# Gated linear attention within chunks: 64x64 blocks on row and column tiles, the inner levels collected at half width

## The chip, the cores and the metric

One core of a Trainium2 chip runs the whole layer in one launch. The metric is device time in microseconds (us), the median of several executions. Before the change it is 1183.76 us (three runs, 1183.09 to 1184.44).

## The reference, cut to what matters

The kernel computes one layer: a token mixer (gated linear attention, GLA, beside a short convolution), an output projection, and a convolutional FFN. The change concerns the attention within chunks of the GLA. For a forward and a backward direction the reference has, with `b` the running sum of the log decays of a chunk:

```python
decay = jnp.exp(jnp.where(mask, b[:, :, None] - b[:, None, :], -jnp.inf))
att = jnp.einsum('bihk,bjhk,bijhk->bijh', qc, kc, decay)
o_intra = jnp.einsum('bijh,bjhv->bihv', att, vc)
```

The decay depends on the channel `k`, so `att` is no single matmul of q and k. There are 1024 tokens, 4 heads, 64 key channels and 128 value channels a head. The kernel works in chunks of 128 tokens.

## The kernel before, in words

**Levels.** A pair of tokens (i, j) of one chunk belongs to the level s of `LEVELS` = 64, 32, 16, 8, 4, 2, 1 at which i and j lie in two neighbouring blocks of s tokens; pairs with i = j are an eighth level, 0. At its own level, the decay from j to i is split at the border of the two blocks into a factor for q and one for k. `level_prep` (L859) makes, for one half of the tokens (4 chunks, 512 columns) and one level, the scaled operands `ql` (tile eq) and `kl` (tile ek): four differences on VectorE (DVE, L867, L868, L875, L876), two exponentials on ScalarE (ACT, through the helper `act`, L127), a product of eq with q on DVE (L882), and the product of ek with k in four parts on GpSimd (POOL, L881). The level with s = 1 needs eq alone, level 0 neither. Tiles eq, ek and eb share a tag with four buffers, so that one level's operands can be made while the level before is multiplied.

**Matmuls.** `level_dot` (L885) multiplies a level: for each of two pairs of chunks (`cp_`) eight matmuls (L894), one for each chunk, each half `fb` of the four heads and each head `hh` in it, with 64 channels on the contraction side and a full block of 128x128 tokens as result. Heads with `hh` 0 and 1 lie on partitions 0 to 63 and 64 to 127, and write two PSUM banks. A result of 128x128 contains products that belong to other levels. The first level is copied whole by ACT into the tile att; each later one is laid over it by a masked copy (`copy_predicated`, DVE, L901), in which the mask of the level picks its own pairs. `out` (L922) then multiplies att with v (L927) and the scaled q with the state (L928), squares on ACT, reduces on DVE, and scales.

**Order.** The order on PE (TensorE) is that of the program. Two generators take turns: `gla` (the attention) and `stream` (blocks of 128 columns of the input projection; "S" below, L144 to L146, 128x512 matmuls on weights in a high and a low part). Each `yield` of the one is followed by one step of the other, twelve S matmuls. A level gives two yields, one after each pair of chunks. Weights of the stream are loaded by the queue of SyncE (SP), copied to their high part wh on ACT and to their low part wl on POOL in four pieces (L634), one block ahead. Beside that run on DVE the recurrence of the states (`recur`, L850, updates of the tile su, 64x128 each, four a chunk) and the short convolution (sc, L676 to L687). The order on DVE, ACT and POOL in this stage is made by a scheduler from the program's order and dependencies; once made, each of these engines runs its own queue in order.

**Stages.** The stage treated here has two halves of tokens (`hf`). Each half runs eight levels and then four `out` steps. Ahead of it the decays are summed (with the matrices tri) and the chunk updates made; behind it follow the last S matmuls, the output projection (w_out) and the FFN.

## Time and profile before

| what | us |
|---|---|
| median of three runs | 1183.76 |
| profiled execution | 1187.9 |
| its span, first to last instruction | 1186.1 |
| levels of the first half, window 247.1 to 317.4 | 70.3 |
| outputs of the first half, to 335.9 | 18.5 |
| levels of the second half, to 401.0 | 65.1 |
| outputs of the second half, to 420.0 | 19.0 |
| L894 busy in the first and the second half's levels | 19.99 and 18.45 |
| masked copies L901 busy in the same windows | 19.23 and 18.88 |

The windows were set by hand at the first matmul of the first level and of the first output of each half. A row of the timeline has start, length, engine, line, operation, output and inputs, shape and count; entries of one kind that follow each other are merged, and in square brackets stands how long the engine was idle before, and who released it. A row of instructions by tile or line has the shortest, median and longest duration in ns. Names are those of the program's tiles without buffer numbers. PEld is the loading of weights into TensorE, PE the matmuls.

### The profile page before, as it was taken

How to read it: one execution, taken by the hardware profiler on the slowest of the kernel's cores; microseconds unless marked ns; L12 is line 12 of the kernel's file. 1: busy time of each engine (PE TensorE's matmuls, PEld its weight loads, DVE VectorE, ACT ScalarE, POOL GpSimd, SP SyncE). 2: the span in 40 equal slices, each digit the busy share in tenths (PEclk: the TensorE clock that was granted, in tenths of full speed). 3: DMA queues.
4: the chain of work that ended last, by engine and by line, in shares of the span. 5: the costliest groups of instructions: out<-in, count | busy, mean ns of one | idle time of the engine just before them, and what ended most of it. 6: DMA issues, size and time to landing. Idle time of an engine off the chain costs nothing. (4 is left out here: it accounts for less than half of the span.)

```text
span 1186.1 us, 15908 instructions
## 1 busy us (share of the span) xinstructions
PE 1150.9 (97%) x5770; PEld 946.1 (80%) x5770; DVE 878.3 (74%) x1215; ACT 518.5 (44%) x931; POOL 479.0 (40%) x467
## 2 busy tenths in 40 slices
PE   8899999999999979999999999999999999999997
PEld 6689967877887868888787788888888888888885
DVE  4965547898769445559688987878787887777676
ACT  5745155643234145556343333333434254544453
POOL 3111001334355201114877776877686871000002
PEclk9999999999999989999999999999999999999999
DMA  9884854311102163232233442233223259978672
GB/s 347 269 293 136 266 153 134 121 57 46 54 18 75 60 217 129 107 125 71 76 101 100 134 141 71 90 125 116 85 79 125 95 161 326 361 246 278 215 241 98
DMA packets 80128, 176.19 MB, mean 149 GB/s; under 512 B 9809, under 2 KB 21585, under 8 KB 80050
## 3 DMA queue, kind: packets, MB, share of 16 engines
q1 hardware_dynamic: 80050, 175.19, 44.4%
q8 instruction: 45, 0.74, 0.3%
q14 instruction: 33, 0.27, 0.1%
HBM read 142.38 MB, written 32.78 MB: 148 GB/s over the span
## 5 line engine op out<-in xcount | busy, mean ns | idle before, releaser
L1296 DVE SCALAR_TENSOR_TENSOR y<-u,cols,y 128x945 f32<-128x945 f32 (+2 forms) x176 | 214.8, 1222 | 3.7 <-ACT y L127 1.3
L144 PE MATMUL ps<-mx,p 128*128 128x512 f32 x440 | 173.6, 395 | 2.9 <-ACT p L127 1.7
L145 PE MATMUL ps<-mx,p 128*128 128x512 f32 x440 | 173.0, 393 | 0.0
L146 PE MATMUL ps<-mx,p 128*128 128x512 f32 x440 | 172.7, 392 | 0.0
L134 POOL TENSOR_TENSOR p<-rs,p 128x512 fp32r<-128x512 f32 x88 | 116.3, 1326 | 88.8 <-ACT p L127 85.0
L146 PE MATMUL ps<-p,p 128*128 128x512 f32 x308 | 120.1, 390 | 0.2
L145 PE MATMUL ps<-p,p 128*128 128x512 f32 x308 | 120.0, 389 | 0.0
L144 PE MATMUL ps<-p,p 128*128 128x512 f32 x308 | 119.9, 389 | 0.0
L634 POOL TENSOR_TENSOR wl<-wr,wh 128x256 fp32r<-128x256 f32 x64 | 52.7, 854 | 159.3 <-ACT wh L127 159.2
L144 PE MATMUL ps<-hxh,wh 128*128 128x512 f32 x256 | 107.5, 420 | 0.0
L229 DVE CUSTOM_DVE_ANT_0 ada<-ada,cb 128x1024 f32<-128x1024 f32 x64 | 79.9, 1263 | 34.2 <-DMA ada<-in_ada 34.1
L144 PEld LDWEIGHTS ps<-mx,p 128*128 128x128 f32 x440 | 82.6, 188 | 25.8 <-ACT u L127 5.0
L146 PE MATMUL ps<-hxh,wl 128*128 128x512 f32 x256 | 101.4, 396 | 0.0
L145 PE MATMUL ps<-hxl,wh 128*128 128x512 f32 x256 | 101.0, 394 | 0.0
L146 PEld LDWEIGHTS ps<-mx,p 128*128 128x128 f32 x440 | 82.6, 188 | 18.6
L127 ACT ACTIVATE p<-rs 128x512 fp32r<-128x512 f32 x88 | 54.5, 622 | 98.0 <-POOL rs L1155 98.0
L145 PEld LDWEIGHTS ps<-mx,p 128*128 128x128 f32 x440 | 82.6, 188 | 18.3
L134 POOL TENSOR_TENSOR p<-wr,p 128x512 fp32r<-128x512 f32 x58 | 76.2, 1314 | 13.1 <-ACT p L127 13.1
L127 ACT ACTIVATE y<-u,cols 128x1024 f32<-128x1024 f32 x22 | 26.6, 1210 | 106.1 <-DVE u L1358 106.1
L144 PE MATMUL ps<-b,p 128*128 128x512 f32 x176 | 69.6, 396 | 0.0
L145 PE MATMUL ps<-b,p 128*128 128x512 f32 x176 | 69.4, 395 | 0.0
L146 PE MATMUL ps<-b,p 128*128 128x512 f32 x176 | 69.4, 394 | 0.0
(271 smaller groups left out, 2636.0 us busy)
## 6 DMA issues: line engine op xcount, KB each, us to landing
ada<-in_ada SPq DMA_DIRECT2D x64, 512.0 KB, 4.6
wr<-in_wu SPq DMA_DIRECT2D x48, 512.0 KB, 4.0
h<-hd SPq DMA_DIRECT2D x77, 256.0 KB, 4.3
hd<-h SPq DMA_DIRECT2D x73, 256.0 KB, 2.1
wdr<-in_wd SPq DMA_DIRECT2D x55, 256.0 KB, 4.0
wdr<-in_wd SPq DMA_DIRECT2D x22, 512.0 KB, 6.1
x<-in_x SPq DMA_DIRECT2D x16, 512.0 KB, 5.5
wr<-in_wb SPq DMA_DIRECT2D x16, 512.0 KB, 3.7
```

Source lines behind the costliest of these rows:

```text
L127: return S.activation(o, i, fn, **kw)
L134: (eng or V).tensor_tensor(lo, raw, hi.bitcast(F32), ALU.subtract)
L144: PE.matmul(ps, lh, rh, start=first, stop=False, skip_group_check=more)
L145: PE.matmul(ps, lh, rl, start=False, stop=False, skip_group_check=more)
L146: PE.matmul(ps, ll, rh, start=False, stop=last, skip_group_check=more)
L229: V.tensor_tensor_reduce(raw, raw, cbs[which], 1.0, 0.0, ALU.mult, ALU.add, dst)
L634: eng.tensor_tensor(lo[:, k : k + 2], raw[:, k : k + 2], hi[:, k : k + 2].bitcast(F32), ALU.subtract)
L1296: V.scalar_tensor_tensor(y3[:, ro, co], u3[:, ri, ci], col("wcf", 9 * p + 3 * (dr_ + 1) + dc + 1), y3[:, ro, co], ALU.mult, ALU.add)
```

## The change

The result of a level is no longer made as 128x128 blocks. Each block is cut into four of 64x64, and only those are computed that the level has pairs in: for level 64 the two off the diagonal (tokens j in one half of the chunk, i in the other), for all others the two on it. One matmul has 64 channels, 64 key tokens and 64 query tokens; the channels' partitions select one of two row tiles of the array, the half `b` of the key tokens one of two column tiles and the output partitions 0 to 63 or 64 to 127. All 32 matmuls of a level are one group, followed by two yields, so 24 S matmuls stand between two groups where 12 stood between two half groups.

The two banks of a level are now full with useful blocks of half width. Level 64 is copied by ACT in four copies of 64 partitions to its places in att; level 32 is copied by ACT whole into a new tile own, which holds the diagonal blocks at half width; the six levels below are laid over own by masked copies, two a half and level; after the last level `whole` copies own into the diagonal places of att in four ACT copies. The masks shrink to 6x64 columns. tri moves from the pool pkq to pgt, which is released at the second step of `kx_turn`, before the first load of the output weights.

```diff
-                for cp_ in range(2):
-                    pts = [bank(ps_at if cp_ == 0 else ps_mm) for _ in range(2)]
...
-                                PE.matmul(pts[hh][:, o : o + P], kl[r, fb, cs], ql[r, fb, cs], start=True, stop=True)
...
-                            V.copy_predicated(dst, masks[:, li - 1, :].unsqueeze(1).broadcast_to([P, H, P]), src)
-                    yield
+            def level_dot(li, kl, ql, att, own):
+                pts = [bank((ps_at, ps_mm)[li % 2]) for _ in range(2)]
+                for n in range(8):
+                    c, fb = n // 2, n % 2
+                    for b in range(2):
+                        ks, qs = (slice(c * P + DK * i, c * P + DK * i + DK) for i in (b, b if li else 1 - b))
+                        for hh in range(2):
+                            r = slice(hh * DK, hh * DK + DK)
+                            PE.matmul(pts[hh][b * DK : b * DK + DK, n * DK : n * DK + DK], kl[r, fb, ks], ql[r, fb, qs],
+                                      start=True, stop=True)
+                for hh in range(2):
+                    src = pts[hh].rearrange("p (a n t) -> p a n t", a=2, t=DK)
+                    if li > 1:
+                        m = masks[:, li - 2, :].unsqueeze(1).unsqueeze(1).broadcast_to([P, 2, 4, DK])
+                        V.copy_predicated(own[:, :, hh], m, src)
+                    elif li == 1:
+                        act(own[:, :, hh], src)
+                    else:
+                        for b in range(2):
+                            r = slice(b * DK, b * DK + DK)
+                            act(att[r, :, hh, :, (1 - b) * DK : (2 - b) * DK], src[r])
+
+            def whole(att, own):
+                for b in range(2):
+                    r = slice(b * DK, b * DK + DK)
+                    for a in range(2):
+                        act(att[r, a, :, :, b * DK : b * DK + DK], own[r, a])
...
-                    yield from level_dot(li, *cur, atts)
+                    level_dot(li, *cur, att, own)
+                    yield
...
+                    if li == len(levels) - 1:
+                        whole(att, own)
+                    yield
```

Where this moves instructions: On PE, in the first level of the first half, eight matmuls of the attention (L894) stood together before S went on; the last two and the first three of S (one hh writes the bank ps_2432, the other ps_2433):

```order
L894 MATMUL ps_2432<-eq_2382,ek_2386 128x128
L894 MATMUL ps_2433<-eq_2382,ek_2386 128x128
L144 MATMUL ps_2404<-hxh_516,wh_2264 128x512
L145 MATMUL ps_2404<-hxl_517,wh_2264 128x512
L146 MATMUL ps_2404<-hxh_516,wl_2265 128x512
```

At the same place of PE's order in the changed kernel, where 32 stand together (all lines lie one or two lower in the file):

```order
L896 MATMUL ps_2432<-eq_2382,ek_2386 64x64
L896 MATMUL ps_2433<-eq_2382,ek_2386 64x64
L145 MATMUL ps_2404<-hxh_516,wh_2264 128x512
L146 MATMUL ps_2404<-hxl_517,wh_2264 128x512
L147 MATMUL ps_2404<-hxh_516,wl_2265 128x512
```

The S matmuls of the same bank follow a group four times as long, of blocks a quarter the size; the second group of eight, which stood behind the next twelve S, is gone.

On DVE, in the first half, the place of level 16's operands (third level; eq_2491 before, eq_2505 now) among the updates of the states su and the convolution's sc. Before:

```order
L854 SCALAR_TENSOR_TENSOR su_1933<-su_1933,dec 64x128 x4
L854 SCALAR_TENSOR_TENSOR su_1932<-su_1933,dec,su_1932 64x128 x4
L854 SCALAR_TENSOR_TENSOR su_1932<-su_1932,dec 64x128 x4
L854 SCALAR_TENSOR_TENSOR su_1931<-su_1932,dec,su_1931 64x128
L686 TENSOR_TENSOR sc_2312<-sc_2312,ps_2404 128x512
L854 SCALAR_TENSOR_TENSOR su_1931<-su_1932,dec,su_1931 64x128 x3
L854 SCALAR_TENSOR_TENSOR su_1931<-su_1931,dec 64x128
L867 TENSOR_TENSOR eq_2491<-bc_1712 128x32x16
```

Now, behind the same first row, where eq_2598 is the fourth level's operand:

```order
L868 TENSOR_TENSOR eq_2505<-bc_1712 128x32x16
L869 TENSOR_TENSOR eq_2505<-bc_1713 128x32x16
L876 TENSOR_TENSOR ek_2509<-bc_1712 128x32x16
L877 TENSOR_TENSOR ek_2509<-bc_1713 128x32x16
L855 SCALAR_TENSOR_TENSOR su_1932<-su_1933,dec,su_1932 64x128
L687 TENSOR_TENSOR sc_2312<-sc_2312,ps_2404 128x512
L883 TENSOR_TENSOR eq_2505<-eq_2505,qh_698 128x1024
L855 SCALAR_TENSOR_TENSOR su_1932<-su_1933,dec,su_1932 64x128 x3
L855 SCALAR_TENSOR_TENSOR su_1932<-su_1932,dec 64x128 x4
L855 SCALAR_TENSOR_TENSOR su_1931<-su_1932,dec,su_1931 64x128 x4
L855 SCALAR_TENSOR_TENSOR su_1931<-su_1931,dec 64x128
L868 TENSOR_TENSOR eq_2598<-bc_1712 128x64x8
```

Level 16's differences moved ahead of thirteen su updates, one of which now stands ahead of their product and twelve between the product and the differences of level 8.

On ACT, at the copies of the first two levels of the first half, behind the copies of ps_2432 and ps_2433 into att. Before:

```order
L127 ACTIVATE att_2418<-ps_2458 128x512
L127 ACTIVATE att_2418<-ps_2459 128x512
L127 ACTIVATE eq_2491<-eq_2491 128x1024
L127 ACTIVATE ek_2495<-ek_2495 128x1024
L127 ACTIVATE wh_2544<-wr_2542 128x1024
L127 ACTIVATE eq_2572<-eq_2572 128x1024
L127 ACTIVATE ek_2576<-ek_2576 128x1024
```

Now, where eq_2505 and ek_2509 are the third level's operands and eq_2598 and ek_2602 the fourth's:

```order
L128 ACTIVATE eq_2505<-eq_2505 128x1024
L128 ACTIVATE ek_2509<-ek_2509 128x1024
L128 ACTIVATE own_2418<-ps_2518 128x2x256
L128 ACTIVATE own_2418<-ps_2519 128x2x256
L128 ACTIVATE eq_2598<-eq_2598 128x1024
L128 ACTIVATE wh_2578<-wr_2576 128x1024
L128 ACTIVATE ek_2602<-ek_2602 128x1024
```

The stream's copy wh moved from between the third and the fourth level's exponentials to between the two exponentials of the fourth. On POOL nothing changes place: the four pieces of wl still stand between the ek products of the third level and those of the fourth.

More of the change, by code (lines that the diff above doesn't have):

```diff
@@ L920, in out_prep, with out @@
                 return qx
-            def out(c, qx, atts):
+            def out(c, qx, att):
                 c4 = c % 4
@@ L926, in out @@
                     hs = slice(h * DV, (h + 1) * DV)
[L927 removed]
+                    PE.matmul(po[:, hs], att[:, c4 // 2, h % 2, 2 * (c4 % 2) + h // 2, :], vt[c][:, hs], start=True, stop=False)
                     PE.matmul(po[:, hs], qx[:, h, :], slot(c)[:, hs], start=False, stop=True)
@@ L945, in gla @@
                     wo_raw(5)
-                atts = [pe_.tile([P, 2, 2, 2, P], F32, tag="att", bufs=2, name=nm("att")) for _ in range(2)]
+                att = pe_.tile([P, 2, 2, 4, P], F32, tag="att", bufs=1, name=nm("att"))
+                own = pe_.tile([P, 2, 2, 4, DK], F32, tag="own", bufs=1, name=nm("own"))
                 for li in range(len(levels)):
@@ L964, in gla @@
                         nxt = level_prep(1, levels[0])
-                    out(4 * hf + c4, qx, atts)
+                    out(4 * hf + c4, qx, att)
                     qx = qn
```

25 lines of the change are left out of this document (6 added, 19 removed).

## The prediction

> **What bounds the kernel now.** I began with the page: span, busy times, and the row of granted clock.
>
> ```profile
> span 1186.1 us, 15908 instructions
> PE 1150.9 (97%) x5770; PEld 946.1 (80%) x5770; DVE 878.3 (74%) x1215; ACT 518.5 (44%) x931; POOL 479.0 (40%) x467
> PEclk9999999999999989999999999999999999999999
> ```
>
> PE carries the kernel, and in the slice that starts at 267 us the clock dips. The change touches only the GLA stage, so the next view is the table by stage: the eight levels of the first half of the tokens, its outputs, the eight levels of the second half, its outputs.
>
> ```profile
> 247.10:317.40 70.30, 67.91 (x449) 53.20 (x449) 63.74 (x104) 23.19 (x26) 30.62 (x41) 0.95 0.16 46
> 317.40:335.90 18.50, 18.50 (x115) 16.12 (x115) 10.41 (x18) 6.20 (x9) 8.01 (x13) 1.00 0.09 29
> 335.90:401.00 65.10, 65.10 (x455) 51.06 (x456) 49.50 (x70) 21.30 (x25) 30.11 (x39) 1.00 0.20 58
> 401.00:420.00 19.00, 19.00 (x115) 16.70 (x114) 9.22 (x17) 4.22 (x7) 5.25 (x8) 1.00 0.25 70
> ```
>
> The columns after the length are PE, PEld, DVE, ACT, POOL, then clock, DMA share and GB/s. PE is full in the second half (65.10 of 65.10) and nearly so in the first; DVE is at 63.74 of 70.30 there. So time that PE saves comes off the end, as long as DVE, ACT and POOL deliver the next level's operands in time. The timeline of PE shows how one group of the attention stands in the stream of 128x512 matmuls ("S" from here on).
>
> ```profile
> 343.84 1.16 PE L894 MATMUL ps<-eq,ek 64*128 64x128 f32 x16
> 344.93 0.50 PE L144 MATMUL ps<-hxh,wh 128*128 128x512 f32 x1
> 345.27 0.39 PE L145 MATMUL ps<-hxl,wh 128*128 128x512 f32 x1
> ...
> 347.56 0.39 PE L146 MATMUL ps<-hxh,wl 128*128 128x512 f32 x1
> 347.88 1.16 PE L894 MATMUL ps<-eq,ek 64*128 64x128 f32 x16
> ```
>
> Ten S steps lie between 345.27 and 347.56, 0.229 us each, twelve are 2.75 us. A group recurs every 4.04 us (343.84 to 347.88), so the eight matmuls of L894 cost 1.29 us. The trace has two entries for each of them (x16). One entry lasts 272 ns (row below), so the 16 start within 1.16 - 0.27 = 0.89 us, 0.056 us apiece; the other 0.40 us is the turn from S to the attention's form and back.
>
> ```profile
> L894 PE MATMUL ps<-eq,ek x384: 272/272/579, 247.1 to 381.1; 64*128 64x128 f32 x192
> 317.88 0.39 PE L927 MATMUL ps<-v,att 128*128 128x128 f32 x2
> 318.10 0.39 PE L928 MATMUL ps<-su,qx 128*128 128x128 f32 x2
> ```
>
> L927 and L928 use all 128 rows: one matmul of two entries each 0.22 us (317.88 to 318.10), 0.11 us an entry, twice the 0.056 us of L894. The two 64-row halves therefore already run side by side, and an entry takes as long as 128 columns need.
>
> The first half has one stall, in the timeline of PE, and it is paid twice:
>
> ```profile
> 259.18 1.16 PE L894 MATMUL ps<-eq,ek 64*128 64x128 f32 x16
> ...
> 265.69 2.60 PE L894 MATMUL ps<-eq,ek 64*128 64x128 f32 x16 [2.40 <-DVE att L901]
> ...
> 273.08 1.16 PE L894 MATMUL ps<-eq,ek 64*128 64x128 f32 x16
> ```
>
> From 259.18 to 265.69 is 6.51 us, 2.47 over the 4.04, a wait for masked copies in DVE's full queue that free the PSUM banks. From 265.69 to 273.08 is 7.39, another 3.35 over, since the clock went down behind the gap (next fence). The stall costs **5.8 us**.
>
> ```profile
> 260.00:270.00 10.00, 7.61 (x40) 6.10 (x37) 9.96 (x15) 3.17 (x4) 6.23 (x8) 0.78 0.11 28
> 270.00:280.00 10.00, 10.00 (x61) 7.71 (x60) 9.20 (x14) 4.73 (x5) 3.55 (x6) 0.88 0.18 53
> ```
>
> **The change, part by part.** *Matmuls.* A level becomes one group of 32 matmuls (64 entries) instead of two of 8 (32 entries). The four 64x64 tiles are two row tiles times two column tiles. The trace shows row tiles side by side and no column tiles, so an entry is bounded: 0.014 us if all four run at once and time goes with columns (half of 0.056 for half the columns, half again for the second pair), and 0.056 us if PE can start none faster than the trace ever shows. I take 0.014, because the row pair runs fully side by side and 128-column entries show no fixed cost beyond their columns: two entries of one 128-column matmul take 0.22 us, an S step of four times the columns 0.229. Then the 64 entries take 0.89 us, and with one turn of 0.40 a level costs 1.29 us instead of 2.58: **16 levels x 1.29 = 20.6 us less**. The level's period goes from 8.08 to 24 x 0.229 + 1.29 = 6.79 us.
>
> Against this stands a rule of the Trainium skill, "TensorE: Matmul & The Clock Gate", section "Back-to-back issue gap": matmuls of 1 to 64 columns follow one another no closer than about 25 ns. By it 64 entries would take 1.6 us, an estimate from that page, and a level 2.0 instead of 1.29; the time is given with the second rival below.
>
> *Evictions.* By level and half four copies become two:
>
> ```profile
> L901 DVE COPY_PREDICATED att<-masks,ps x56: 716/730/747, 264.8 to 398.2; 128x512 f32<-128x512 uint8 x56
> L127 ACT ACTIVATE att<-ps x8: 577/590/598, 248.3 to 343.2; 128x512 f32<-128x512 f32 x8
> L127 ACT ACTIVATE su<-ps x14: 573/592/597, 217.0 to 246.3; 64x512 f32<-64x512 f32 x14
> ```
>
> The 56 masked copies become 24 of the same 512 elements, so DVE loses 32 x 0.73 = 23.4 us. ACT gets 8 copies of 64x512 for level 0 (as many as before; 0.59 by the su row), 4 of 0.59 for level 1 and 8 of about 0.59 that put the diagonal blocks into att: 12 x 0.59 = 7 us on an engine that is busy 23.19 of 70.30. I cost these at nothing. The last four stand between the last level and the first output matmul: two masked copies and four ACT copies are 1.46 + 2.36 = 3.8 us, beneath 24 S steps (5.5 us). If DVE came over 1.7 us late to them, PE would wait for the rest.
>
> *The old stall* goes: level 1's copies are ACT's now, so level 2's successors no longer wait for DVE's queue. **5.8 us less.**
>
> *What is late next.* Level 3's ek. In DVE's queue level 2's four differences and product now come right behind the su update that ended at 254.95, and twelve su updates stand between them and level 3's. Durations:
>
> ```profile
> 253.77 1.18 DVE L854 SCALAR_TENSOR_TENSOR su<-su,dec 64x128 f32<-64x128 f32 x4
> ...
> 257.40 0.69 DVE L686 TENSOR_TENSOR sc<-sc,ps 128x512 f32<-128x512 f32 x1
> ...
> 259.30 0.69 DVE L867 TENSOR_TENSOR eq<-bc 128x512 f32<-128x512 f32 x1
> ...
> 261.72 1.23 DVE L882 TENSOR_TENSOR eq<-eq,qh 128x1024 f32<-128x1024 f32 x1
> ```
>
> ```profile
> L854 DVE SCALAR_TENSOR_TENSOR su<-su,dec 64x128 f32<-64x128 f32 x20 | 8.7, 506 | 0.1
> L854 DVE SCALAR_TENSOR_TENSOR su<-su,dec,su 64x128 f32<-64x128 f32 x16 | 5.3, 393 | 0.0
> ```
>
> An su update is (8.7 + 5.3) / 36 = 0.39 us, four differences 261.72 - 259.30 = 2.42. So: 254.95 + 2.42 + 0.39 + 0.69 + 1.23 = 259.7, + 12 x 0.39 = 264.4, + 2.42 = 266.8, when level 3's ek differences are ready. On ACT, wh now stands between level 3's two exponentials, and on POOL the four wl of that wh still stand ahead of level 3's ek:
>
> ```profile
> 261.89 1.06 ACT L127 ACTIVATE ek<-ek 128x1024 f32<-128x1024 f32 x1 [0.20 <-DVE ek L876]
> 262.85 1.04 ACT L127 ACTIVATE wh<-wr 128x1024 fp32r<-128x1024 f32 x1
> ```
>
> ```profile
> 263.03 3.03 POOL L881 TENSOR_TENSOR ek<-ek,kh 128x256 f32<-128x256 f32 x4 [10.12 <-ACT ek L127]
> 266.01 3.24 POOL L634 TENSOR_TENSOR wl<-wr,wh 128x256 fp32r<-128x256 f32 x4
> 272.26 2.80 POOL L881 TENSOR_TENSOR ek<-ek,kh 128x256 f32<-128x256 f32 x4 [3.00 <-ACT ek L127]
> ```
>
> The eq exponential starts with the second difference (265.6) and ends at 266.6, wh at 267.7, wl at 270.9; the ek exponential is done at 268.7 and waits. The group's second matmul pair needs the third of four ek parts: 270.9 + 2.27 = 273.2. PE is due at 247.1 + 3 x 6.79 = 267.5. **A new stall of 5.7 us, and 3.35 for the clock behind it: 9.0 us more.** In the second half the same chain has no su updates, 4.7 us less: 5.7 - 4.7 = 1.0 us more, too short a gap, I take it, to move the clock (the gap that did was 2.40). The Trainium skill, same page, section "HAM oscillation — how this bites in real kernels", puts that limit at idle gaps of over about 3.4 us; the trace disagrees, the 2.40 us above was followed by 0.78.
>
> Both ends: without any new stall it is 10.0 us better; if wl and contention add as much again as the second half's 1.0 in each later level, some 6 worse.
>
> *Masks and tri.* The smaller mask load and its cast, and tri's place among the buffers that are released before the first wo load, lie ahead of the levels beside full PE work: nothing.
>
> *After the stage* the S stream ends with the outputs as now, and the w_out start waits for a chain that begins at that end:
>
> ```profile
> 439.76 0.80 PE L144 MATMUL ps<-woh,mh 128*128 128x512 f32 x1 [6.53 <-ACT mh L127]
> ```
>
> So it moves along whole. **Sum:** 20.6 + 5.8 - 9.0 - 1.0 = 16.4 us. The profiled execution took 1187.9 us (span 1186.1), 4.1 over the median shown, so it would take 1171.5, and the median of 1183.76 goes to **1167.4**.
>
> **Rivals.** *No new stall* (su updates shorter, or wh early): 20.6 + 5.8 = 26.4, 1157.4. For it: DVE loses 23.4 us; against: the queue's order.
>
> *Column tiles take turns*: row pairs side by side, but the two column tiles of one row pair one after the other, 32 steps of 0.056 = 1.79 us, a level 2.19. Gain 16 x 0.39 = 6.2; level 3 is due at 270.2, stall 3.0 + 3.35; 6.2 + 5.8 - 6.4 = 5.6, **1178.2**. For it: no row shows column tiles at once. By the 25 ns of the Trainium skill's page above, a level of 2.0 would give about 1175.6, an estimate.
>
> *Slower: PE starts entries no faster than now.* Place: PE's own issue of 64 short entries a level; price 64 x 0.056 + 0.40 = 3.98 a level, 16 x 1.40 = 22.4 us more, less the 5.8 of the old stall (level 3, due at 275.5, finds its ek): 16.6 more, **1200.4**. It decides from 16 x (x - 2.58) = 5.8, a level of 2.94 us or 40 ns an entry. For it: 0.056 is the closest spacing of the trace, and the entries double. Against: that spacing is explained by columns alone. This is also the case in which the change doesn't do what it says.
>
> **How the numbers follow.** Forecast 1167.4: 0.50 (own range 1162 to 1173). No new stall, 1157 to 1162: 0.11. Column tiles in turn or a start every 25 ns, 1174 to 1180: 0.23. Slower: 0.16. The range 1157 to 1180 leaves out the slower case. A measurement of this kernel tells 0.2%, 2.4 us, from no change: slower 0.16; between the second rival and the slower one, same 0.04; faster 0.80.
>
> **What would show it.** A group of 64 entries: about 1.1 us long in the timeline if all four tiles run, 2 us in turn, 3.8 if issue-bound. PE's wait before level 3 of the first half, named for POOL's ek at L882, with a clock dip behind it; none before level 2. Masked copies x24 at 0.73. What would make it wrong: a 64x64 entry spaced over 40 ns, a wait of the outputs for ACT's att copies, or masked copies that take longer on four-level operands than 0.73.

## The result, and the profile after

The changed kernel takes **1173.18 us** (median of six runs, 1170.04 to 1174.74) where the kernel before takes 1183.67 (six runs, 1182.38 to 1185.46). The ratio is 0.9903, 95% interval [0.9885, 0.9922]: 9.2 to 13.6 us less. 1167.4 had been forecast, within 1157 to 1180; the median lies 0.2 us above the narrower range that the forecast gave itself, 1162 to 1173. The profiled execution took 1172.66 us. Three rows of its page, the span, the engines and the granted clock:

```profile
span 1170.7 us, 16901 instructions
PE 1129.3 (96%) x6282; PEld 930.1 (79%) x6282; DVE 870.4 (74%) x1183; ACT 524.8 (45%) x943; POOL 490.8 (42%) x467
PEclk9999999998999989999999999999999999999999
```

PE is busy 21.6 us less (1150.9 before), but the span is only 15.4 us shorter. The table by stage shows where PE now stands still; its columns are those of the same table before.

```profile
242.90:305.60 62.70, 57.69 (x705) 46.04 (x705) 60.15 (x88) 25.38 (x31) 34.40 (x39) 0.95 0.18 51
305.60:324.00 18.40, 18.40 (x117) 16.04 (x117) 11.35 (x18) 7.31 (x11) 8.62 (x13) 1.00 0.11 32
324.00:383.80 59.80, 55.21 (x706) 44.22 (x706) 42.67 (x54) 25.07 (x31) 32.86 (x36) 1.00 0.22 62
383.80:402.80 19.00, 19.00 (x117) 16.81 (x116) 9.40 (x16) 4.02 (x8) 8.22 (x12) 1.00 0.27 72
```

Both halves' levels got shorter, 70.3 to 62.7 us and 65.1 to 59.8, and both outputs stayed as they were. PE waits 5.0 us in the first half and 4.6 in the second, which had no wait before. PE's timeline of the first half (L896 is the level's matmul, and 64 entries are now one group; levels are counted by their place from 0 on, so level 3 is the one with s = 8):

```profile
242.92 1.16 PE L896 MATMUL ps<-eq,ek 64*64 64x64 f32 x64
249.68 1.16 PE L896 MATMUL ps<-eq,ek 64*64 64x64 f32 x64
254.56 0.47 PE L145 MATMUL ps<-hxh,wh 128*128 128x512 f32 x1 [0.77 <-ACT ek L128]
257.46 1.56 PE L896 MATMUL ps<-eq,ek 64*64 64x64 f32 x64
267.88 0.34 PE L896 MATMUL ps<-eq,ek 64*64 64x64 f32 x8 [3.16 <-POOL ek L882]
269.25 2.06 PE L896 MATMUL ps<-eq,ek 64*64 64x64 f32 x56 [1.03 <-POOL ek L882]
278.66 1.16 PE L896 MATMUL ps<-eq,ek 64*64 64x64 f32 x64
```

An undisturbed level takes 249.68 - 242.92 = 6.76 us; a group's entries start within 1.16 - 0.22 = 0.94 us. Level 3 is the one that waits: 3.16 us ahead of its group, and again after eight entries, when the part of ek that the next one needs isn't there. From 267.88 to 278.66 is 10.78 us, 4.0 over an undisturbed level, of which 1.03 is that second wait; the rest is the clock, at half speed up to 275 and full from there:

```profile
268.20:274.90 6.70, 5.67 (x69) 4.57 (x66) 6.70 (x9) 2.49 (x3) 3.50 (x5) 0.50 0.22 75
275.00:280.00 5.00, 5.00 (x82) 3.99 (x81) 5.00 (x5) 3.43 (x4) 5.00 (x5) 1.00 0.02 3
```

The view of waits over both halves names one releaser for nearly all of it:

```profile
PE ps L896 <- POOL ek L882: 8.8, 8, 3.2
```

The other 0.77 us, at 254.56, is put down to ACT's ek, which S does not read. By the program's order S goes on there to a new bank, the one that ps_2404 had before, and the last to read ps_2404 is sc on DVE (L687). That row ends 0.15 us earlier, so it is most likely what S waited for:

```profile
253.73 0.69 DVE L687 TENSOR_TENSOR sc<-sc,ps 128x512 f32<-128x512 f32 x1
```

How level 3's ek came to be late, in the timelines of DVE, ACT and POOL:

```profile
260.69 0.69 DVE L868 TENSOR_TENSOR eq<-bc 128x512 f32<-128x512 f32 x1
...
262.02 1.06 ACT L128 ACTIVATE eq<-eq 128x1024 f32<-128x1024 f32 x1 [6.45 <-DVE eq L869]
262.99 1.05 ACT L128 ACTIVATE wh<-wr 128x1024 fp32r<-128x1024 f32 x1
263.94 1.04 ACT L128 ACTIVATE ek<-ek 128x1024 f32<-128x1024 f32 x1
...
264.11 2.98 POOL L635 TENSOR_TENSOR wl<-wr,wh 128x256 fp32r<-128x256 f32 x4 [5.73 <-ACT wh L128]
267.05 3.28 POOL L882 TENSOR_TENSOR ek<-ek,kh 128x256 f32<-128x256 f32 x4
```

That is the chain of the forecast, in its order: the differences behind the su updates, wh between the two exponentials, the four wl ahead of the product. For the second half, three of its products of ek and k and a wl between them, in POOL's timeline:

```profile
344.48 4.12 POOL L882 TENSOR_TENSOR ek<-ek,kh 128x256 f32<-128x256 f32 x4
351.60 3.73 POOL L882 TENSOR_TENSOR ek<-ek,kh 128x256 f32<-128x256 f32 x4 [3.00 <-ACT ek L128]
355.29 4.77 POOL L635 TENSOR_TENSOR wl<-wr,wh 128x256 fp32r<-128x256 f32 x4
360.02 4.06 POOL L882 TENSOR_TENSOR ek<-ek,kh 128x256 f32<-128x256 f32 x4
```

The product takes about 4 us at levels 2 to 5 here. In the second half before the change its four pieces took 2.8, as in this row of POOL's timeline of before:

```profile
357.94 2.83 POOL L881 TENSOR_TENSOR ek<-ek,kh 128x256 f32<-128x256 f32 x4 [3.00 <-ACT ek L127]
```

PE waits 0.27, then 0.92, 1.48 and 0.44 at one level, and 1.31 and 0.18 at another, all for POOL's ek. Counted over both traces, 85% of the time of the second half's products lies beside DVE instructions that read two operands from SBUF, where it was 6% before (70% and 21% in the first half), and a piece takes 1.05 us on average instead of 0.74.

### The profile page after: what moved, and what is told of

It reads as the page before. It is cut to its first block, busy times and chain, and to the rows that moved or that the text cites. A ratio compares the mean times of both kernels' runs of the same rounds, so it can differ in the third digit from the quotient of the medians.

```text
span 1170.7 us, 16901 instructions
## 1 busy us (share of the span) xinstructions
PE 1129.3 (96%) x6282; PEld 930.1 (79%) x6282; DVE 870.4 (74%) x1183; ACT 524.8 (45%) x943; POOL 490.8 (42%) x467
## 5 line engine op out<-in xcount | busy, mean ns | idle before, releaser
L635 POOL TENSOR_TENSOR wl<-wr,wh 128x256 fp32r<-128x256 f32 x64 | 57.1, 921 | 160.3 <-ACT wh L128 159.0
L135 POOL TENSOR_TENSOR p<-wr,p 128x512 fp32r<-128x512 f32 x58 | 76.2, 1313 | 13.1 <-ACT p L128 13.1
```

Of the source, the lines that this page charges most:

```text
L135: (eng or V).tensor_tensor(lo, raw, hi.bitcast(F32), ALU.subtract)
L635: eng.tensor_tensor(lo[:, k : k + 2], raw[:, k : k + 2], hi[:, k : k + 2].bitcast(F32), ALU.subtract)
```

## The experiments

Two theories stood at the start. The first, that of the prediction: the new waits are the operands' chain DVE, ACT, POOL, which no longer keeps up with a level of 6.76 us. The second: the matmuls' new form or grouping costs something by itself. Later the question was which link of the chain it is. The table gives, for every kernel that ran, its time, and from its profiled execution the first half's levels (first entry of level 0 to the first output matmul), the outputs behind them, the second half's levels, and the sum. The six runs of the changed kernel alone differ by 4.7 us, and the profiled executions begin the stage at 239.5 to 247.1 us, so the verdicts go by the stage. The texts of the first runs give the second half of the changed kernel as 60.6 us, up to a mark 0.8 us later; in the table it is 59.83.

| kernel | time, us | first half | outputs | second half | sum |
|---|---|---|---|---|---|
| before | 1183.67 | 70.37 | 18.32 | 64.56 | 153.25 |
| changed | 1173.18 | 62.69 | 18.32 | 59.83 | 140.84 |
| e1 columns in turn | 1177.36 | 66.68 | 18.32 | 61.30 | 146.30 |
| e2 two groups | 1173.38 | 63.47 | 18.43 | 59.96 | 141.86 |
| e3 no ek product | 1156.91 | 53.99 | 18.34 | 54.00 | 126.33 |
| e4 su later | 1176.49 | 64.79 | 19.19 | 61.89 | 145.87 |
| e5 product on DVE | 1166.40 | 60.78 | 20.03 | 54.00 | 134.81 |
| e6 product shared | 1165.69 | 62.56 | 18.43 | 55.18 | 136.17 |
| e7 level 1 on DVE | 1171.41 | 64.50 | 18.32 | 59.78 | 142.60 |
| e8 no wl | 1155.42 | 56.05 | 18.32 | 54.61 | 128.98 |
| e9 wl behind | 1170.54 | 62.07 | 18.43 | 58.97 | 139.47 |
| e10 shared, wl behind | 1168.44 | 62.50 | 18.43 | 55.16 | 136.09 |
| e11 su spread | 1169.42 | 59.91 | 20.76 | 58.36 | 139.03 |
| e12 combined | 1172.05 | 63.96 | 21.66 | 56.99 | 142.61 |

Before, changed and e12 are medians of six; the others one run each, with the kernel before at 1181.45 to 1183.53 beside them. The stage is measured in one execution of each, and part of it is the clock: in the three parts of the table it was at half speed for no time in e2, e3 and e8, for 3.4 us in e6, e9, e10 and e11, twice 3.4 in e5 and e7, 6.8 in before, changed, e1 and e12, and 6.8 and 3.4 in e4. Half of such a stretch is lost when PE is busy. Sums that differ by less than 3 us therefore decide little by themselves; the waits named below decide more.

**e1: the column tiles one after the other.** All entries of one column tile, then all of the other.

```diff
-                for n in range(8):
-                    c, fb = n // 2, n % 2
-                    for b in range(2):
+                for b in range(2):
+                    for n in range(8):
+                        c, fb = n // 2, n % 2
```

> The changed kernel with one thing else: the 32 matmuls of a level run through all eight blocks on column tile 0 first and on column tile 1 after that, so that no two neighbours in the queue differ in the column tile. In the changed kernel a group's 64 entries start within 0.94 us. Theory A (column tiles run side by side when they stand next to each other): 0.94 grows to about 1.8 us, and the levels of the two halves (62.7 and 60.6 us) by up to 7 us each, less where a wait for ek is there anyway. Rival (the entries are short because they have half the columns, and PE takes them from far ahead in its queue or never needed column tiles): the group stays at 0.94 to 1.0 us.

PE's timeline of this kernel, its first two groups:

```profile
242.84 1.91 PE L896 MATMUL ps<-eq,ek 64*64 64x64 f32 x64
250.36 1.91 PE L896 MATMUL ps<-eq,ek 64*64 64x64 f32 x64
```

The entries now start within 1.91 - 0.22 = 1.69 us and a level takes 7.52 instead of 6.76. The single starts in the traces show why. Before the change they come in pairs 7 ns apart, a pair every 112 ns; in e1 in pairs every 59 ns, for half the columns; in the changed kernel in fours 7 ns apart, a four every 59 ns, one entry for each tile. So the two column tiles do run side by side in the changed kernel, where entries for the one and the other stand next to each other, and do not where all of one come first; whether the matmul or the loading of its weights sets the 59 ns isn't separated. The 1.79 us of the prediction's second rival was the price of the order it hadn't got. Sixteen levels cost 12.2 us more, but the stage only 5.5: PE is later at each level and waits less for ek.

**e2: two groups of 32 entries a level**, with twelve S between them, as many groups as before the change.

```diff
                 for n in range(8):
+                    if n == 4:
+                        yield
...
-                    level_dot(li, *cur, att, own)
-                    yield
+                    yield from level_dot(li, *cur, att, own)
```

> The changed kernel with a level's matmuls in two groups of 16 again, twelve S matmuls between them; blocks, tiles and evictions as in the changed kernel. Theory A (the new waits come from when ek is made, behind DVE's and POOL's queues, not from the grouping): one turn more a level, 16 x 0.32 to 0.40 = 5 to 6 us more on PE, of which waits for ek swallow some; the levels take 62 to 66 us in the first half and 60 to 64 in the second. Theory B (the waits come from needing all four parts of ek at once): the waits shrink by more than the turns cost, and both halves are shorter than 62.7 and 60.6 us, by 2 us or more each.

The entries of a group start within 0.47 us and one more turn is paid a level, 16 x 0.38 = 6.1 us; yet the stage is 1.0 us longer only. PE waits some 2 us less, and the clock stays at 1.00 (the longest wait is 1.56 us), where the changed kernel lost about 3 us to it. As long as POOL is late, one group a level was worth 1 us here; how often the clock would fall in further runs isn't known.

**e3: without the product of ek and k** (the levels use ek as the exponential left it).

```diff
-                for fb in range(2):
-                    for q in range(2):
-                        part = slice(q * 256, q * 256 + 256)
-                        G.tensor_tensor(kl[:, fb, part], kl[:, fb, part], kh[hf][:, fb, part], ALU.mult)
```

> The changed kernel without POOL's product of ek with k (levels 64 to 2 multiply the bare exponential): this part of the computation is left out. Theory A: PE waits for that product, 8.7 us in the first half (with the clock behind it) and 5.8 in the second; without it both halves come near 8 x 6.76 = 54.1 us, the first within 3 us of it (DVE's queue), the second within 1, and the kernel gains 10 to 14 us. Rival (DVE's queue is what is late, POOL only the last link): the first half stays above 59 us.

The table by stage of this kernel for its two halves' levels:

```profile
242.90:296.90 54.00, 54.00 (x706) 43.78 (x706) 51.68 (x86) 24.19 (x30) 11.90 (x14) 1.00 0.19 58
315.00:369.00 54.00, 54.00 (x706) 43.66 (x705) 35.66 (x53) 24.86 (x31) 13.59 (x17) 1.00 0.22 68
```

PE is full, 8 x 6.75 us in each half, at full clock. All 14.5 us that the changed kernel loses in the stage are gone with this one product, and the matmuls' new form or grouping makes no wait of its own. DVE, with the same work but no product beside it, reaches level 3's differences 13.1 us after the stage's start; in the changed kernel it takes 17.8.

**e4: the su updates later**, two levels behind their place, DVE in the order of the program up to level 6 of the first half.

```diff
-                    if hf == 0 and li < NT - 1:
-                        recur(li, True)
-                        if li < 3:
-                            recur(li, False)
+                    if hf == 0 and 2 <= li < NT - 1:
+                        for n in ((0, 1), (2, 3), (4,), (5,), (6,))[li - 2]:
+                            recur(n, True)
+                        if li < 5:
+                            recur(li - 2, False)
```

> The changed kernel with the su updates of the first half put two levels later and DVE in program order there, so that no su update stands between level 2's and level 3's differences. Theory A (those updates make level 3 late): the first half falls from 62.7 us to 57 or less with no wait of over 1 us before its fourth group and no clock dip; the second half stays at 60.6 within 1. Rival (wl in POOL's queue alone makes ek late): the first half stays above 60 us.

PE's timeline where it now waits:

```profile
263.40 1.16 PE L896 MATMUL ps<-eq,ek 64*64 64x64 f32 x64
270.53 0.34 PE L896 MATMUL ps<-eq,ek 64*64 64x64 f32 x8 [0.30 <-POOL ek L882]
...
281.62 0.34 PE L896 MATMUL ps<-eq,ek 64*64 64x64 f32 x8 [2.67 <-POOL ek L882]
```

Level 3 (263.40) has no wait any more, as far as the updates were its cause. But level 5 got one of 2.67, and the half is 2.1 us longer: the rival's number, though wl alone is not what the runs below show. The updates decide which level is late, not whether one is. The second half, expected unchanged, is 2.1 us longer, with waits of 4.8 us in all against 4.6; the clock fell there (last section).

**e5: the product on DVE.**

```diff
-                for fb in range(2):
-                    for q in range(2):
-                        part = slice(q * 256, q * 256 + 256)
-                        G.tensor_tensor(kl[:, fb, part], kl[:, fb, part], kh[hf][:, fb, part], ALU.mult)
                 V.tensor_tensor(ql, ql, qh[hf], ALU.mult)
+                V.tensor_tensor(kl, kl, kh[hf], ALU.mult)
```

> The product of ek and k of levels 1 to 7 moves from POOL (four pieces, 2.8 to 4.5 us in the changed kernel's trace) to DVE, one instruction behind the product of eq and q, 1.23 us as that one. Theory A (the new waits are the POOL product itself: its length beside DVE, the wl ahead of it in POOL's queue, and what it takes from DVE): the second half loses its waits, 59.83 to 54 to 55 us, since DVE was busy 35.7 us of 54 there with the product left out and gets 8.6 more; in the first half DVE was busy 51.7 of 54 with the product left out, so with 8.6 more DVE itself sets the length, 58 to 61 us (62.69 in the changed kernel); no wait of PE is named for POOL; about 1164 us, 1160 to 1168. Theory B (DVE's queue in the first half, with twelve su updates ahead of level 3's differences, is what makes level 3 late, POOL only passes it on): DVE gets 2.5 us more ahead of level 3, its wait grows from 3.2 us to over 5, the first half is 63 us or longer, about 1171.

Theory A held: the second half has no wait left (54.00), the first is 60.78. Its longest wait, in PE's timeline (L893 is the level's matmul there), and the clock behind it, in a table by windows:

```profile
273.92 1.16 PE L893 MATMUL ps<-eq,ek 64*64 64x64 f32 x64 [2.38 <-DVE ek L880]
...
274.00:283.00 9.00, 9.00 (x136) 7.24 (x140) 9.00 (x12) 3.07 (x3) 3.34 (x4) 0.81 0.21 60
```

The wait has gone from POOL to DVE, which is full (9.00 of 9.00). A second one, 1.82 us ahead of the first output, is for `whole`, since DVE came late to the last masked copies; the 3.4 us at half clock behind it make the outputs 1.7 us longer.

**e6: the product shared**, POOL the first 512 columns, DVE the others.

```diff
-                for fb in range(2):
-                    for q in range(2):
-                        part = slice(q * 256, q * 256 + 256)
-                        G.tensor_tensor(kl[:, fb, part], kl[:, fb, part], kh[hf][:, fb, part], ALU.mult)
+                for q in range(2):
+                    part = slice(q * 256, q * 256 + 256)
+                    G.tensor_tensor(kl[:, 0, part], kl[:, 0, part], kh[hf][:, 0, part], ALU.mult)
                 V.tensor_tensor(ql, ql, qh[hf], ALU.mult)
+                V.tensor_tensor(kl[:, 1], kl[:, 1], kh[hf][:, 1], ALU.mult)
```

> The product of ek and k is shared: POOL does the first 512 columns of each partition (two pieces, 1.4 us undisturbed), DVE the other 512 (0.68 us) behind the product of eq and q. Theory A (as above, each engine's time adds up): POOL's part is half as long and DVE gets 7 x 0.68 = 4.8 us in a half; first half 56 to 59 us, second half 54 to 56, about 1161 to 1164 us, no longer than the kernel with the whole product on DVE. Theory B (the place in POOL's queue behind the four wl, not the product's length, makes it late): level 3 of the first half still waits 2 us or more for POOL, and the second half keeps 2 us or more of its 5.8; about 1167 us or more.

The second half fell as theory A has it, to 55.18. The first did not: PE waits 3.14 us for POOL ahead of level 3, as theory B has it, though the product is half as long. POOL's timeline shows what stands ahead of it:

```profile
262.24 3.38 POOL L635 TENSOR_TENSOR wl<-wr,wh 128x256 fp32r<-128x256 f32 x4 [6.00 <-ACT wh L128]
265.58 1.51 POOL L881 TENSOR_TENSOR ek<-ek,kh 128x256 f32<-128x256 f32 x2
```

**e7: level 1's copies back on DVE**, one part of the change undone.

```diff
                     elif li == 1:
-                        act(own[:, :, hh], src)
+                        V.tensor_copy(own[:, :, hh], src)
```

> Undoes one part: the two copies of level 1's result from PSUM are DVE's again (plain copies, 0.7 us each by the masked ones), at the place that DVE's queue gives them, in the first half behind the su updates and ahead of level 3's differences. If the old stall went because level 1's copies became ACT's, as the prediction has it: in the first half PE waits ahead of level 2, for banks, until DVE comes to them at about 260.7 to 262 (254.6 in the changed kernel): a wait of 6 to 8 us, the clock low behind it, the wait for level 3's ek gone or under 1 us since everything is later; first half 66 to 70 us, about 1177 to 1181 us. Rival (the stall went because there are half as many groups and copies, whoever makes them): no wait over 1.5 us ahead of level 2, level 3's wait longer by the two copies' 1.4 us, about 1174 to 1175 us.

PE's timeline has the wait, but at another place and much smaller:

```profile
262.22 0.50 PE L145 MATMUL ps<-hxh,wh 128*128 128x512 f32 x1 [1.41 <-DVE own L904]
268.18 0.34 PE L896 MATMUL ps<-eq,ek 64*64 64x64 f32 x8 [2.93 <-POOL ek L882]
```

PE comes to the bank only after level 2's group, 1.41 us ahead of DVE, not at 254, and no low clock follows there. The first half is 1.8 us longer, not 3 to 7. The rival isn't right either: level 3's wait did not grow (2.93). DVE's copies cost a wait of 1.41 us where the old stall had 2.40, so the prediction's reason for its end (level 1's copies are ACT's now) holds for a part of it at most. What else differs is that a level needs its two banks once instead of twice, so copies have longer before PE is back at them; that is argued, no run separates it further.

**e8: without wl** for the blocks 3 to 17 of the stream.

```diff
-            lo = wp.tile([P, KT, P], F32R, tag="wlo", name=nm("wl"))
+            lo = first_lo[0] if first_lo else wp.tile([P, KT, P], F32R, tag="wlo", name=nm("wl"))
             act(hi, raw)
-            for k in range(0, KT, 2):
+            for k in range(0, 0 if first_lo else KT, 2):
```

> Leaves out the low part wl of the weight blocks 3 to 17 of the stream (all matmuls run, with block 2's low part), so POOL has only the product of ek and k in the levels. Theory A (the wl ahead of the product in POOL's queue is what makes it late at level 3 of the first half, and at the levels of the second half where a wl stands next to it): level 3's wait of 3.2 us falls under 0.5 with the low clock behind it, first half 55 to 58 us (62.69), and at least 3 of the 5.8 us go in the second half, 54 to 57 us; about 1163 us. Rival (the product alone, 2.8 to 4.5 us beside DVE, is too long for the chain of a level): waits of 3 us or more remain in each half, about 1168 us or more.

Level 3 keeps 0.69 us, level 4 0.44, the second half 0.39: theory A, but for the 0.5 it gave level 3. The time, 1155.42, is 8 us under the 1163 expected; 3.5 of that are that the stage begins earlier. With e3 this makes a pair. Without the product 14.5 us go, without wl 11.9, of 14.5 that there are. They don't add up: as far as these two runs show, POOL and DVE manage either load within a level, not both.

**e9: wl behind the product**, nothing left out. The low part of a block is made half a block later, and POOL's order in the levels follows the program.

```diff
-                nxt = block(3 + n) if n < 15 else None
+                nxt = high(3 + n) if n < 15 else None
...
+                for step, _ in enumerate(halves(w, dests)):
+                    if step == 1 and nxt:
+                        nxt = low(*nxt)
+                    yield
...
+                        byhand = tc.manual_schedule(engines={mybir.EngineType.Pool})
+                        byhand.__enter__()
```

> Nothing is left out and nothing is moved to another engine: only POOL's order in the levels is written by hand, so that the wl of a block is issued half a block later than now and stands behind the product of ek and k of the next level (in the first half behind level 3's, where the changed kernel has it ahead). Theory A (it is the place of wl in POOL's queue): level 3's wait of 3.2 us falls under 1 us, and with it the low clock behind; first half 56 to 59 us (62.69), second half 55 to 57.5 (59.83), about 1165 us. Theory B (it is the work itself: wl takes the port from DVE and the product runs at 4 us beside DVE wherever wl stands): the stall only moves to a later level; first half over 61, second over 58.5, 1170 to 1174 us.

PE's timeline of the first half:

```profile
265.51 0.34 PE L914 MATMUL ps<-eq,ek 64*64 64x64 f32 x8 [1.28 <-POOL ek L900]
266.98 1.27 PE L914 MATMUL ps<-eq,ek 64*64 64x64 f32 x56 [1.12 <-POOL ek L900]
...
276.16 0.69 PE L914 MATMUL ps<-eq,ek 64*64 64x64 f32 x32 [1.18 <-POOL ek L900]
```

Level 3 waits 1.3 us ahead of its group and 1.1 in it, instead of 3.2 and 1.0, and level 4 has a new wait: 62.07 and 58.97 us, theory B. The place of wl explains which level is late, as the su updates do; that one is late at all fits the sum of work, which e3, e5 and e8 made smaller.

**e10: e9 and e6 together**, with e6's edit.

> The kernel before it (wl behind the product in POOL's queue), and the product shared by POOL and DVE as in the earlier run, where level 3 of the first half waited 3.1 us for POOL's half behind the four wl. Theory A (that wait was wl's place): it falls under 1.2 us (DVE's own half is done at 264.0 there and PE due at 263.3); first half 56 to 59 us (62.56 when shared with wl ahead), second half 54 to 55; about 1160 to 1163 us. Theory B (DVE's queue sets the first half, 51.7 us with no product, and 4.8 more): the first half stays over 60, about 1164 to 1166 us.

Level 3's wait fell to 0.82, as theory A has it. Yet the half took 62.50, over theory B's 60, by a wait that neither theory had named. It is in PE's and ACT's timelines:

```profile
274.46 0.61 PE L145 MATMUL ps<-hxh,wh 128*128 128x512 f32 x1 [3.64 <-ACT sc L128]
...
272.87 1.06 ACT L128 ACTIVATE eq<-eq 128x1024 f32<-128x1024 f32 x1 [7.81 <-DVE eq L887]
273.83 0.58 ACT L128 ACTIVATE sc<-ps 128x512 f32<-128x512 f32 x1
```

S needs a bank that ACT has to empty; that copy stands in ACT's queue behind an exponential which waits for DVE's differences. DVE's lateness reaches PE through ACT's queue, without POOL.

**e11: e10 with the su updates spread**, DVE's order in the first half by hand.

```diff
+            SU_AT = {0: [(0, True)], 1: [(1, True)], 3: [(0, False)], 4: [(2, True)], 5: [(3, True), (1, False)],
+                     6: [(4, True), (5, True), (2, False)], 7: [(6, True)]}
...
-                        recur(li, True)
+                        for n, back in SU_AT.get(li, ()):
+                            recur(n, back)
```

> The kernel before it, and DVE's order in the first half by hand: of the su updates four stand behind each of levels 0, 1, 3 and 4, eight behind level 5, twelve behind level 6 and four behind level 7, in place of twelve between level 2's product and level 3's differences. With the product whole on POOL, moving them later only moved the stall. Theory A (that was POOL's load; with POOL relieved, DVE's order is what is left): level 3's operands are ready 3 to 4 us earlier, no wait over 0.7 us, first half 54 to 56.5 us, second half as in the kernel before it; about 1158 to 1161 us. Theory B (DVE is simply full in the first half, so the place of the updates does not matter): first half within 1 us of that of the kernel before it, or longer, since an order by hand makes DVE wait for others.

PE's timeline has no wait up to level 5; then these two:

```profile
284.77 1.16 PE L914 MATMUL ps<-eq,kh 64*64 64x64 f32 x64 [1.33 <-DVE eq L890]
...
302.72 0.79 PE L957 MATMUL ps<-v,att 128*128 128x128 f32 x2 [4.37 <-ACT att L128]
```

What was taken from the early levels turned up at level 6 and at the outputs, where `whole` waits for masked copies that DVE comes to late. First half and outputs together are 80.67 us, 80.93 in e10: theory B for the sum, though the first half alone is 2.6 shorter. The second half, with the same code, is 3.2 us longer than in e10. Of these, 2.2 are waits, the longest 1.63 us of S for a bank that sc on DVE (L704) empties; why they came in this run stays open.

**e12: the parts combined**: e11 with the su updates at other places (eight ahead of level 0; behind levels 5 to 7 they are 24 as in e11, but twelve of them behind level 7), and in the second half the product whole on DVE.

```diff
+                        recur(0, True)
+                        recur(0, False)
...
+            SU_AT = {0: [(1, True)], 1: [(2, True)], 5: [(3, True), (1, False)], 6: [(4, True)],
+                     7: [(5, True), (6, True), (2, False)]}
...
+                if hf:
+                    V.tensor_tensor(ql, ql, qh[hf], ALU.mult)
+                    V.tensor_tensor(kl, kl, kh[hf], ALU.mult)
+                    return kl, ql
```

> Brings together what the runs left standing. First half: the product of ek and k shared by POOL and DVE, wl behind it in POOL's queue, DVE's order by hand with the su updates thinner at its end than in the run with them spread (eight ahead of level 0's group, four behind levels 0 and 1, none up to level 4, eight behind level 5, four behind 6, twelve behind 7), which had its first six levels without a wait and then lost 1.3 us ahead of the last level but one and 4.4 us at the first output, where DVE came late to the last masked copies. Second half: the whole product on DVE, which had no wait there. Theory A (each stall has its own cause in the operands' chain, and DVE's load fits once it is spread): first half 54 to 56.5 us, second half 54 to 55, outputs between them 18.3 to 19.5, about 1159 to 1162 us. Theory B (DVE is full in the first half and what is taken from one level turns up at another): first half or the outputs behind it longer by 4 us or more, 1164 to 1168 us.

1172.05 us (six runs), ratio to the kernel before 0.9918 [0.9904, 0.9933]: no better than the changed kernel, theory B again and over its 1164 to 1168, and worse than the changed kernel by the stage, 142.61. In DVE's, POOL's and PE's timelines an early loss and a late one can be seen:

```profile
248.72 3.03 DVE L873 SCALAR_TENSOR_TENSOR su<-su,dec,su 64x128 f32<-64x128 f32 x4
...
249.32 3.03 POOL L651 TENSOR_TENSOR wl<-wr,wh 128x256 fp32r<-128x256 f32 x4
...
302.11 1.32 DVE L924 COPY_PREDICATED own<-masks,ps 128x512 f32<-128x512 uint8 x2
...
305.30 0.79 PE L961 MATMUL ps<-v,att 128*128 128x128 f32 x2 [5.72 <-ACT att L128]
```

Four su updates take 3.03 us beside POOL's wl (1.17 where POOL is idle, in the changed kernel at 249.63), and level 2 waits 1.81. The larger loss is at the end: the last level's group began at 292.75, but DVE came to its masked copies only at 302.11, and PE waited 5.72 us for the first output, with 6.8 us at half clock behind. The three kernels with the shortest stages and nothing left out are e5, e10 and e6, 1166.40, 1168.44 and 1165.69 us. Each lies below all six runs of the changed kernel, but each ran once, so a version that beats both kernels is likely here and not measured with an interval.

## Why the prediction came out as it did

**The matmuls: right.** Forecast 1.29 us a level instead of 2.58, 20.6 us in all; measured 8.08 to 6.76, 16 x 1.32 = 21.1. The spacing of 0.014 us an entry is 0.94 / 63 = 0.015. The choice between the bounds 0.014 and 0.056 went by columns alone, and e1 shows the condition that came with it unsaid: matmuls for the two column tiles must stand close to each other in the queue. The choice came out, but its second reason was weak: an entry of 128 columns at 0.11 us against an S step of 512 at 0.229 is half the time for a quarter of the columns, which does not exclude a fixed cost. That it is small shows only now: 59 ns for 64 columns after 112 for 128 leave 2 x 59 - 112 = 6 ns. Turn-taking, the rival, would have cost 0.75 us a group (e1). The Trainium skill's 25 ns from start to start ("TensorE: Matmul & The Clock Gate", section "Back-to-back issue gap") would make a group of 64 take 1.6 us, an estimate; the trace has 0.94.

**The evictions at nothing: right.** The outputs take 18.32 us before and after, and the 24 masked copies take 0.73 us each. The condition that was named with it, DVE late at the last copies, cost waits of 1.82 us in e5, 4.37 in e11 and 5.72 in e12. DVE's gain did not come in full: its copies fell from 38.1 to 16.2 us in the four windows, but its other instructions there rose from 94.8 to 107.4.

**The old stall gone: right in size** (no wait for masked copies is left; the one of 0.77 us is most likely for a bank that sc on DVE empties), **in part only in its reason** (e7). The digit 8 that the prediction places at 267 us is the slice at 415 us, behind the wait at 439.76; the dip itself is in the windows at 260 and 270 that it shows.

**The new stall at level 3: right in place, chain and size.** Counted from the stage's start, the differences were forecast at 264.4 - 247.1 = 17.3 us and came at 17.8, and the third part of ek was forecast at 26.1 and came at about 26.3, when the group went on. Forecast 9.0 us more for the first half; it is 62.69 - 8 x 6.76 = 8.6 over its undisturbed length. That it is so close is in part luck: PE came to level 3 later than reckoned, 0.77 us of it by the wait at 254.56, so the stall itself is 3.16 + 4.0 = 7.2, and the rest was lost before it. What the runs add is why the chain is that late: not the order alone (e4, e9), but what POOL's product and wl take from DVE while they run (e3: 13.1 us to the differences instead of 17.8).

**The second half: the term that was mis-sized.** "In the second half the same chain has no su updates, 4.7 us less: 5.7 - 4.7 = 1.0 us more." It is 59.83 - 54.08 = 5.75 us more. The step took the chain at level 3 with durations of before and left the other levels out. In fact the product takes 3.7 to 4.5 us there instead of 2.8, at every level from 2 to 5: levels follow each other faster, and 85% of its time now lies beside DVE instructions with two SBUF operands, 6% before. e5 (product on DVE: 54.00), e3 and e8, in which one of the loads is taken away, show that it is this. The prediction had it in its upper bound only ("contention ... some 6 worse").

**The sum.** 21.1 + 5.7 - 8.6 - 5.8 = 12.4 us in the stage, against 16.4 forecast. The profiled execution is 15.2 us shorter because its stage also began 4.1 us earlier (242.92 against 247.06), through work ahead of the levels (up to 1.7 us of it by 3.4 us at half clock at 180, which only the trace of before has; the rest wasn't followed), while what lies behind the stage took 1.2 longer (786.93 against 785.76 from the second outputs on). The medians differ by 10.5, with the 12.4 inside the interval.

**The rivals.** No new stall fell. Column tiles in turn fell for the order written, and was priced well for the other: e1's group has 1.69 us where 1.79 was worked out, and e1 took 1177.36 where 1178.2 was. The slower case needed 40 ns an entry; there are 15.

## What to carry to other kernels

Where PE gets faster in a loop, time the chain of operands of every turn against the new period, with durations as they are when the engines of the chain work side by side, not those of a looser loop. If one level is late, move its work once; if the stall then only turns up at another level (the su updates, wl), it is the load of the chain, and only taking work out of it, or to an engine with room, helps. Matmuls on 64x64 tiles should be written so that the column tiles take turns at short distance; here that was 0.94 us a group against 1.69.

## What the runs showed of the hardware

**What POOL costs DVE depends on the operands.** In DVE's timeline of the changed kernel, second half, beside the POOL pieces shown above (351.60 to 360.06):

```profile
353.51 1.22 DVE L869 TENSOR_TENSOR eq<-bc 128x512 f32<-128x512 f32 x1
...
355.80 0.67 DVE L687 TENSOR_TENSOR sc<-sc,ps 128x512 f32<-128x512 f32 x1
356.40 0.68 DVE L877 TENSOR_TENSOR ek<-bc 128x512 f32<-128x512 f32 x1
```

A difference of two SBUF operands takes 0.68 us alone and mostly 1.22 beside POOL; a product of the same size with one operand from PSUM takes 0.67 beside POOL. The difference at 356.40 began 0.03 us ahead of a piece of POOL and took 0.68; there the piece took 1.24 us instead of 0.73. So either of the two can be the one that is held up. The Trainium skill, "GPSIMD Engine Reference", section "Specifications", says that GpSimd shares its SBUF interfaces with VectorE and contends with DVE instructions that have two SBUF inputs; the trace agrees with it, in the product with a PSUM operand too, which is not slowed.

**The clock falls after shorter gaps than expected, and not by their length alone.** It went to 0.50, for 3.4 or 6.8 us, behind each single wait of 1.90 us or more in the stage (the shortest in e7 and e9, 1.90 and 1.93 us). Below that it varied: it fell behind one of 1.82 (e5) and not behind one of 1.81 (e12). The limit of about 3.4 us in the Trainium skill, "TensorE: Matmul & The Clock Gate", section "HAM oscillation — how this bites in real kernels", isn't what these traces show. The waits of 0.92, 1.48 and 0.44 in the second half of the changed kernel had no fall behind them; in e4, 0.90, 1.48 and 0.44 at the same level had one (there 0.71 and 0.44 had gone before, at level 2). Rows of the changed kernel and of e4, by windows behind the last of these waits, the first number after the counts being the clock:

```profile
348.70:352.00 3.30, 3.30 (x36) 2.75 (x37) 3.30 (x5) 1.53 (x2) 0.40 (x1) 1.00 0.30 84
...
353.90:357.20 3.30, 3.30 (x30) 2.70 (x31) 3.30 (x5) 1.57 (x2) 0.36 (x1) 0.50 0.30 84
```

What decides between them no run here shows.
